# A two-layer hybrid block: the written order counts transfers on the load queue, large loads come in pieces, and the first transfers go through one queue

## The chip, the cores and the metric

The kernel runs on one core of a Trainium2 chip. A core has a matrix engine (TensorE, here PE, with its weight loads shown apart as PEld), a vector engine (VectorE, DVE), an activation engine (ScalarE, ACT), GpSimd (POOL) and SyncE (SP), which in this kernel issues nearly all transfers. Each engine runs its own instructions in the order in which the program wrote them and waits on semaphores for the others. Transfers run on 16 DMA engines. The metric is the device time of one execution in microseconds (us); lower is better. "Granted clock" is the share of its full clock that PE was given.

## The reference: what is computed

Two layers are applied to a sequence of 256 rows of width 1024, then a final RMS norm. A layer normalises its input, projects it with one wide matrix, and runs three branches on the parts:

```
h = rms_norm(x); proj = h @ w_in           # 1024 x 14352
y_a = differential attention: 8 heads, RoPE, causal softmax, a = p0 - lam * p1, norm, * silu(z), @ w_o
y_c = u = a * sigmoid(g); depthwise causal convolution of 31 taps; layer_norm; silu * silu(z); @ w_o
y_d = short convolution of 4 taps, silu, l2 norm; gated delta rule, 8 heads of 128;
      norm, * silu(z), @ w_o
x = x + (g_a * y_a + g_c * y_c + g_d * y_d) @ w_out     # gates: sigmoid of three parts of proj
```

All of it is float32. The gated delta rule solves a unit lower triangular system for each chunk of the sequence and head; the kernel inverts its 16x16 diagonal blocks first and goes on from there with matrix products.

## The kernel before

**Dense products.** All large weights are cut into groups of 512 columns, and each group into four chunks of 512 KB (`w_raw`, 128 partitions x 1024). SP loads a chunk (`load`, L423), ACT rounds it to `w_hi` (`prepare`, L430), DVE takes the rest as `w_lo` (`lows`, L442), and PE multiplies three times: high by high, high by low, low by high. There are three buffers of each of the three tiles. A chunk's load is issued when `w_lo` of the chunk three before it has been taken, since only then is its raw buffer free. `dense` (L477) runs one group: four chunks, and between their matmuls it calls `pump` (L365).

**How the order of the work is set.** The program writes all instructions of a layer in one pass, and a small planner chooses their order. A clock `clk[0]` counts the time of PE's matmuls by fixed costs; `busy` has the time up to which DVE, ACT and GpSimd are filled. Side work is a set of generators, each a `Stream` (L284) with a priority. A stream's `yield` closes a run of steps. `serve` (L301) writes the stream's next step when its inputs should be there by the planner's clock. For a transfer, `dma` (L356) takes a number, the time after which the planner believes that the data has landed, and a plain `yield 8.0` sets the start of the run of steps that it closes 8 us later. For weights, `load` notes `clk[0] + 4.5` as the landing. No two transfers know of each other in this account. Once written, the order is fixed: if a transfer lands later than the planner thought, the engine that needs it stands, and all that is written behind it on that engine stands too.

**The order of groups.** `SEQ` (L60) lists the steps of the projection phase: `v` the attention values, `k` the delta-rule keys, `q` its queries, `w` its values, `x` the start of its solve, `c` the two convolution groups, `d` a block of the long convolution, `a` attention queries and keys, `z` a gate, `t` the RoPE tables. The digit is the half (or the block for `d`). Behind them come, for the delta branch, the attention and the convolution in turn, gate groups (`g`) and output products (`y`) as `PHASE` lists them: for the delta branch g0, g1, y0, y1. The four convolution blocks are 256 channels each: block 0 runs on DVE as scaled adds over time (`conv_steps`, L1132), blocks 1 to 3 on PE (`conv_group`, L1163).

**Block copies.** `dn_keys` (L878) makes the 16x16 diagonal blocks of one half of the heads (`vc`), stores them to DRAM (`v_keep`, 64 KB) and reads them back so that each partition holds all 16 rows of its block: `nrep`, two copies of 512 KB, on a tile named `y_hi` in the first half of the heads and `t8` (shown as `t`) in the second. Then DVE runs the inverse: 15 steps, of which step i reads the rows 0 to i of `nrep`, into `dn_z`, with `dn_t` as room. GpSimd spreads `dn_z` (POOL, `t<-dn_z`), PE transposes it, and the solve goes on. The SP engine waits for the store to land before the copies, as they read what it wrote.

**Convolution loads.** `evac_u` (L1113) makes 512 of the convolution's input channels, stores them to DRAM (`u_keep`, 512 KB) and, for the first half, starts `conv_load(1)` (L1147): the taps as a block of matrices (`wd`, 1 MB), then `u4` (shown as `u`), the input four times, shifted by 0 to 3 steps, 256 KB each, read from `u_keep`. `conv_group(n)` starts `conv_load(n + 1)` when its matmuls have been written.

**The start.** x comes transposed (`xt`, four transfers of 256 KB): three on ACT's queue and one on SP's; the weights come on SP's. ACT issues the transfers of four constants before its first activation. `first_part` (L610) scales two slices of x, `prepare(2)` takes the first chunk in two halves, and then the dense work of the first group begins.

## Time and profile before

| | us |
|---|---|
| median of 3 runs | 1114.2 (1113.66 to 1120.59) |
| profiled execution, its own time | 1114.95 |
| its span, first to last instruction | 1113.2 |
| PE busy | 1044.5 |
| DVE busy | 866.7 |
| ACT busy | 548.3 |
| mean granted clock | 0.971 |

The profile is of one execution. Times in it count from its first instruction. A row of a timeline gives start, length, engine, line, operation and operands; in square brackets stands the idle time of the engine before it and what ended it. "SPq" and "ACTq" are transfers issued by these engines, and their length is that of the issue, not of the transfer. "DMA y_hi<-v_keep" as the end of a wait is the landing of that transfer. A row of the view by stretch gives the stretch, its length, the busy time of PE, PEld, DVE, ACT and POOL (with the number of instructions), the granted clock, the DMA engines' busy share and GB/s. Almost all vector and activation work bears line 130, that of a helper, so the tile names tell it apart.

### The profile page before, as it was taken

Reading aid. Unit: us, or ns where it says so; the run is one execution under the profiler, and the core shown is the slowest. Engines: PE = TensorE matmul, PEld = TensorE weight load, DVE = VectorE, ACT = ScalarE, POOL = GpSimd, SP = SyncE. Lnnn points to the kernel's source line nnn. Section 1 sums busy time; section 2 is a strip of 40 time slices with the busy share of each in tenths; the row PEclk is TensorE's granted clock in tenths of the full one; section 3 lists DMA queues with packets and bytes.
Section 4 is the critical chain, followed back from the end, with each engine's and each line's share of the span. In section 5 each row is a group of like instructions: output and inputs, shape, how many; then the busy total and the mean of one; then the engine's idle time right before and its main releaser. Section 6 shows DMA issues by size and latency. Waiting matters only on the chain.

```text
span 1113.2 us, 18028 instructions
## 1 busy us (share of the span) xinstructions
PE 1044.5 (94%) x6892; PEld 905.1 (81%) x6892; DVE 866.7 (78%) x1729; ACT 548.3 (49%) x977; POOL 102.3 (9%) x73
## 2 busy tenths in 40 slices
PE   6999759989999999999999998998989999999996
PEld 5899747889877888897889998788978777879885
DVE  4799657769766899996578979876877579989855
ACT  4564325334544556554456553534354355665543
POOL 0001001300010000121100200030000000002220
PEclk8999878989999999999999998999989999999998
DMA  6555573244535456556665566634443535645662
GB/s 215 160 163 165 177 191 114 97 135 133 159 111 148 133 172 206 169 187 193 185 206 168 153 197 213 179 114 133 135 134 110 137 117 168 212 150 174 198 207 82
DMA packets 57894, 178.07 MB, mean 160 GB/s; under 512 B 6480, under 2 KB 16336, under 8 KB 57040
## 3 DMA queue, kind: packets, MB, share of 16 engines
q1 hardware_dynamic: 56240, 175.17, 52.0%
q10 hardware_dynamic: 1568, 1.75, 0.5%
q8 instruction: 54, 0.88, 0.3%
q14 instruction: 32, 0.26, 0.1%
HBM read 172.44 MB, written 4.46 MB: 159 GB/s over the span
## 4 chain that ended last, share of the span: by engine, by line
PE 69%; DVE 17%; DMA 8%; issue 3%; ACT 2%; SPq 0%; ACTq 0%; DVEq 0%
PE acc L349 55%; PE s L347 11%; DVE w_lo L130 6%; DMA w_raw<-in_wts 4%; PE s L354 3%; DVE big L130 2%; DMA y_hi<-v_keep 1%; DMA t<-v_keep 1%; ACT w_hi L130 1%; DVE c_acc L130 1%; DVE vv L130 1%; DVE gx L130 1%; DMA big<-in_x_t 1%; DVE dn_t L130 1%; DMA u_keep<-c_u 0%
## 5 line engine op out<-in xcount | busy, mean ns | idle before, releaser
L130 ACT CAST w_hi<-w_raw 128x1024 fp32r<-128x1024 f32 (+1 forms) x289 | 302.3, 1046 | 354.7 <-PE acc L349 235.7
L130 DVE TENSOR_TENSOR w_lo<-w_raw,w_hi 128x1024 fp32r<-128x1024 f32 (+1 forms) x289 | 365.5, 1266 | 77.7 <-ACT w_hi L130 76.8
L349 PE MATMUL acc<-h_hi,w_lo 128*128 128x256 f32 x768 | 220.5, 287 | 14.3 <-DVE w_lo L130 14.1
L349 PE MATMUL acc<-h_hi,w_hi 128*128 128x256 f32 x768 | 224.5, 292 | 0.0
L349 PE MATMUL acc<-w_hi,h_hi 128*128 128x512 f32 x512 | 216.0, 422 | 6.6 <-ACT w_hi L130 6.6
L349 PE MATMUL acc<-h_lo,w_hi 128*128 128x256 f32 x768 | 219.3, 286 | 0.0
L349 PE MATMUL acc<-w_lo,h_hi 128*128 128x512 f32 x512 | 202.0, 395 | 0.6 <-DVE w_lo L130 0.6
L349 PE MATMUL acc<-w_hi,h_lo 128*128 128x512 f32 x512 | 202.2, 395 | 0.0
L349 PEld LDWEIGHTS acc<-h_hi,w_lo 128*128 128x128 f32 x768 | 149.4, 195 | 16.1 <-DVE w_lo L130 15.9
L349 PEld LDWEIGHTS acc<-h_hi,w_hi 128*128 128x128 f32 x768 | 149.7, 195 | 1.4 <-issue 1.0
L349 PEld LDWEIGHTS acc<-h_lo,w_hi 128*128 128x128 f32 x768 | 149.6, 195 | 0.3
L349 PEld LDWEIGHTS acc<-w_hi,h_hi 128*128 128x128 f32 x512 | 97.7, 191 | 26.0 <-ACT w_hi L130 6.8
L349 PEld LDWEIGHTS acc<-w_hi,h_lo 128*128 128x128 f32 x512 | 97.1, 190 | 21.7 <-DVE h_lo L130 0.2
L349 PEld LDWEIGHTS acc<-w_lo,h_hi 128*128 128x128 f32 x512 | 98.0, 191 | 17.0 <-DVE w_lo L130 1.9
L130 DVE SCALAR_TENSOR_TENSOR c_acc<-c_u,pc,c_acc 128x255 f32<-128x255 f32 (+29 forms) x120 | 51.3, 470 | 2.3 <-ACT c_acc L130 2.3
L349 PE MATMUL acc<-w_hi,y_lo 128*128 128x512 f32 x128 | 50.1, 391 | 2.0 <-DVE y_lo L130 2.0
L349 PE MATMUL acc<-w_hi,y_hi 128*128 128x512 f32 x128 | 51.5, 402 | 0.3 <-ACT y_hi L130 0.3
L349 PE MATMUL acc<-w_lo,y_hi 128*128 128x512 f32 x128 | 49.9, 390 | 0.0
L130 DVE SCALAR_TENSOR_TENSOR big<-wc,pc,big 128x255 f32<-128x255 f32 (+2 forms) x96 | 47.6, 543 | 0.5 <-ACT big L130 0.5
L349 PE MATMUL acc<-u,wd 128*32 128x256 f32 (+7 forms) x768 | 41.7, 369 | 1.8 <-ACT c_acc L130 1.8
L349 PE MATMUL acc<-w_hi,t 128*128 128x512 f32 x128 | 40.0, 389 | 0.0
L349 PEld LDWEIGHTS acc<-u,wd 128*32 128x32 f32 x768 | 23.7, 110 | 18.3 <-ACT c_acc L130 3.5
(276 smaller groups left out, 1521.1 us busy)
## 6 DMA issues: line engine op xcount, KB each, us to landing
w_raw<-in_wts SPq DMA_DIRECT2D x287, 512.0 KB, 3.8
wd<-in_cwd SPq DMA_DIRECT2D x6, 1024.0 KB
y_hi<-v_keep SPq DMA_DIRECT2D x4, 512.0 KB
u_keep<-c_u SPq DMA_DIRECT2D x4, 512.0 KB, 5.3
t<-v_keep SPq DMA_DIRECT2D x4, 512.0 KB
u<-u_keep SPq DMA_DIRECT2D x6, 256.0 KB, 6.4
u<-u_keep SPq DMA_DIRECT2D x6, 255.0 KB, 7.3
u<-u_keep SPq DMA_DIRECT2D x6, 254.0 KB, 7.2
```

What stands on the lines that cost most here:

```text
L130: step = (self.key, lambda: getattr(self.eng, op)(*args, **kw), cost)
L347: live[0].steps.append(("PE", lambda: TE.matmul(**kw), cost))
L349: TE.matmul(**kw)
L354: ("PE", lambda: TE.transpose(out=out, in_=in_, identity=ident[0:n, 0:n]), 0.11))
```

## The change

**Account of the queue.** `dma` takes a size and a rate in place of a landing time. `transfer` keeps two times: `lane[0]`, when SP is free to issue (0.45 us an issue), and `lane[1]`, when the queue has moved all that was asked (1.2 us from issue at the earliest, then size by rate, 280 GB/s if nothing else is said); landing is 0.6 us later. Weight loads go through the same account. A stream whose last step is a transfer is done at its landing, so `until` on it waits for that.

**Block copies.** Four copies of 256 KB in place of two of 512 KB, each a stream of its own, written some 1.8 us apart from right behind the store on; the inverse waits for the landing of each quarter before step 4, 8 and 12 (and before its first step for the first). Their rate in the account is 130 GB/s.

**Convolution loads.** `conv_load` is now started behind the second convolution group, at a high priority. The taps come in four transfers of 256 KB, 1.5 us apart; the four shifted inputs are 2 us apart, and begin at the landing of the stored half.

**Order of groups.** `d1`, block 1 of the convolution, stands behind `w1` and `x1`. Block 3 (`last_conv`, L1483) stands behind the delta branch's first product (`y`) instead of its first gate group.

**First transfers.** x and the first chunks go through SP's queue in the order x 0-1, weights 0a, x 2-3, weights 0b, weights 1, x 4-7, weights 2. The four constants are issued by ACT behind its work on the first two chunks.

```
@@ -57,7 +57,7 @@
     PHASE[k] = (("g", 0), ("g", 1), ("y", 0), ("y", 1))
-SEQ = "v0 k0 t0 z0 k1 v1 q0 w0 c0 x0 q1 a0 d1 w1 x1 c1 z1 a1 d2".split()
+SEQ = "v0 k0 t0 z0 k1 v1 q0 w0 c0 x0 q1 a0 w1 x1 d1 c1 z1 a1 d2".split()
 TAPQ = 8
@@ -225,8 +225,6 @@
     xt = act.tile([P, KT, T], F32, name="big", bufs=3)
-    for k in (0, 2):
-        nc.scalar.dma_start(out=xt[:, k:k + 2], in_=x_t[:, k:k + 2])
     S.activation(out=one, in_=ones[:, 0:1], func=AF.Square)
@@ -284,7 +282,7 @@
             self.gen, self.prio, self.steps, self.held, self.marks = gen, prio, [], [], False
-            self.t, self.on, self.over, self.done, self.read = clk[0], "", False, False, None
+            self.t, self.on, self.over, self.done, self.read, self.land = clk[0], "", False, False, None, 0.0
@@ -310,6 +308,7 @@
                         self.done = True
+                        self.t = max(self.t, self.land)
                         streams.remove(self)
@@ -330,7 +329,8 @@
                     else:
-                        self.t = clk[0] + cost
+                        self.land = max(self.land, transfer(due, *cost))
+                        self.t = lane[0]
                     self.on = key
@@ -353,8 +353,16 @@
-    def dma(landing, **kw):
-        live[0].steps.append(("SP", lambda: nc.sync.dma_start(**kw), landing))
+    def dma(kb, rate=280.0, **kw):
+        live[0].steps.append(("SP", lambda: nc.sync.dma_start(**kw), (kb, rate)))
+    def transfer(due, kb, rate=280.0):
+        lane[0] = max(lane[0], due, clk[0]) + 0.45
+        lane[1] = max(lane[1], lane[0] + 1.2) + kb * 1.024 / rate
+        return lane[1] + 0.6
+    lane = [0.0, 0.0]
@@ -420,12 +428,14 @@
-    def load():
+    def load(freed=0.0):
         if len(raws) < len(queue):
...
                 nc.sync.dma_start(out=raw[:, kk], in_=wts[queue[len(raws)]][:, kk])
-            raws.append((raw, clk[0] + 4.5))
+                if not raws and not kk:
+                    nc.sync.dma_start(out=xt[:, 2:4], in_=x_t[:, 2:4])
+            raws.append((raw, transfer(freed, 512)))
@@ -447,7 +457,7 @@
             if kk.stop == KC:
-                load()
+                load(ready[n][2])
@@ -644,15 +654,12 @@
+    nc.sync.dma_start(out=xt[:, 0:2], in_=x_t[:, 0:2])
     load()
-    nc.scalar.dma_start(out=xt[:, 4:6], in_=x_t[:, 4:6])
     load()
-    nc.sync.dma_start(out=xt[:, 6:8], in_=x_t[:, 6:8])
+    nc.sync.dma_start(out=xt[:, 4:8], in_=x_t[:, 4:8])
     load()
-    nc.scalar.dma_start(out=cst[:, 0:CO_NW], in_=consts[:, 0:CO_NW])
-    nc.scalar.dma_start(out=cst[:, CO_TRI:CO_N], in_=consts[:, CO_TRI:CO_N])
-    nc.scalar.dma_start(out=pat, in_=patt)
-    nc.scalar.dma_start(out=pos_i, in_=positions.rearrange("b (c p) -> p (b c)", p=P))
+    lane[0] = lane[1] = 9.5
     idle = side[0][0]
@@ -665,9 +672,13 @@
     prepare()
-    clk[0] = 6.5
+    clk[0] = 6.0
     s_f = add(first_half())
     s_r = [(1, s_f)]
+    nc.scalar.dma_start(out=cst[:, 0:CO_NW], in_=consts[:, 0:CO_NW])
+    nc.scalar.dma_start(out=cst[:, CO_TRI:CO_N], in_=consts[:, CO_TRI:CO_N])
+    nc.scalar.dma_start(out=pat, in_=patt)
+    nc.scalar.dma_start(out=pos_i, in_=positions.rearrange("b (c p) -> p (b c)", p=P))
     s_q = add(first_squares(), 0.1)
@@ -924,22 +935,39 @@
             st["gam"], st["ngam"], st["nk"] = gam, ngam, nk
-            dma(3.5, out=v_keep[hs], in_=vc.rearrange("p c h i -> p (c h i)"))
-            yield 3.5
-            for half in range(2):
-                dma(0.1 if half else 7.0, out=nrep[:, 8 * half:8 * half + 8].rearrange("p j c i -> p (j c i)"),
-                    in_=v_keep[hs].rearrange("(b h j) n -> h b (j n)", b=8, h=2)[half].unsqueeze(1).to_broadcast(
-                        [8, 16, 8 * P]))
-            yield 8.0
+            dma(64, out=v_keep[hs], in_=vc.rearrange("p c h i -> p (c h i)"))
+            yield 0.1
+            def blocks(n):
+                dma(256, 130.0, out=nrep[:, 4 * n:4 * n + 4].rearrange("p j c i -> p (j c i)"),
+                    in_=v_keep[hs].rearrange("(b h j) n -> h b (j n)", b=8, h=4)[n].unsqueeze(1).to_broadcast(
+                        [8, 16, 4 * P]))
+                yield
+            def copies():
+                for n in range(4):
+                    s_b.append(add(blocks(n), 0.05))
+                    yield 1.8
+            s_b = []
+            add(copies(), 0.05)
+            while not s_b:
+                yield
+            yield from until(s_b[0])
             z = sm.tile([P, 8, 16], F32, name="dn_z", bufs=1)
...
             for i in range(1, 16):
+                if i % 4 == 0:
+                    yield
+                    while len(s_b) <= i // 4:
+                        yield
+                    yield from until(s_b[i // 4])
                 t1 = sm.tile([P, 8, 16], F32, name="dn_t1", bufs=1)
...
                 V.tensor_reduce(out=z[:, :, i:i + 1], in_=t1[:, :, 0:i + 1], axis=AX.X, op=ALU.add)
-                if i % 3 == 0 or i == 7:
-                    yield 6.0 if i == 7 else None
+                if i % 4 == 1:
+                    yield
             if hs == 0:
@@ -1117,15 +1145,15 @@
                 yield
-                dma(3.0, out=u_keep[s * GW:(s + 1) * GW].rearrange("(a p) t -> p a t", p=P), in_=us[s])
-                stored.append(s)
+                yield from ()
+                dma(512, out=u_keep[s * GW:(s + 1) * GW].rearrange("(a p) t -> p a t", p=P), in_=us[s])
                 if s == 0 and NV:
                     taps_left[0] = conv_steps()
-                if s == 0 and NV < 2:
-                    s_cv[NV] = add(conv_load(NV))
             s_g = group_a(l, ("in", CG + s * GW), H, evac_g)
-            group_a(l, ("in", CA + s * GW), H, evac_u)
+            stored.append(group_a(l, ("in", CA + s * GW), H, evac_u))
+            if s == 0 and NV < 2:
+                s_cv[NV] = add(conv_load(NV), 0.05)
@@ -1145,13 +1173,19 @@
         def conv_load(n):
-            dma(0.1, out=wd.rearrange("p f q j c -> p (f q j c)"), in_=cwd[l, n - NV])
+            for f in range(2):
+                for q in range(2):
+                    qs = slice(4 * q, 4 * q + 4)
+                    dma(256, out=wd[:, f, qs].rearrange("p q j c -> p (q j c)"),
+                        in_=cwd[l, n - NV].rearrange("p (f q x) -> p f q x", f=2, q=2)[:, f, q])
+                    yield 1.5
             while len(stored) <= n // 2:
                 yield
-            yield 3.0
+            yield from until(stored[n // 2])
             for i in range(4):
-                dma(0.1 if i < 3 else 6.0, out=u4[32 * i:32 * i + 32, :, i:T],
+                dma(256, 150.0, out=u4[32 * i:32 * i + 32, :, i:T],
                     in_=u_keep[n * 2 * P:(n + 1) * 2 * P, 0:T - i].rearrange("(g c) t -> c g t", c=32))
+                yield 2.0
@@ -1176,7 +1210,7 @@
             if n < 3:
-                s_cv[n + 1] = add(conv_load(n + 1))
+                s_cv[n + 1] = add(conv_load(n + 1), 0.05)
@@ -1481,7 +1515,7 @@
         def last_conv(kind, i):
-            if kind == "g" and not i:
+            if kind == "y" and not i:
                 conv_group(3)
```

## The prediction

> **What bounds the kernel now.** I read the totals of the page first, then the stretches in which TensorE (PE) stands still, then who it waits for, then the load queue. The totals:
>
> ```profile
> PE 1044.5 (94%) x6892; PEld 905.1 (81%) x6892; DVE 866.7 (78%) x1729; ACT 548.3 (49%) x977; POOL 102.3 (9%) x73
> ```
>
> PE is the bound over most of the span, so only what PE loses can be won. The view of busy time by stretch shows where it loses it (stretch, its length, then PE busy first; granted clock, DMA share and GB/s last). These seven stretches hold the larger gaps behind the start:
>
> ```profile
> 124.00:132.00 8.00, 1.31 (x9) 1.10 (x8) 3.17 (x9) 1.04 (x1) 0.00 (x0) 0.71 0.33 109
> 150.00:170.00 20.00, 5.58 (x19) 3.94 (x18) 8.65 (x16) 5.33 (x9) 2.41 (x2) 0.62 0.45 123
> 240.00:246.00 6.00, 1.97 (x14) 1.77 (x13) 1.73 (x8) 3.36 (x14) 0.00 (x0) 0.78 0.53 144
> 665.00:673.00 8.00, 1.48 (x10) 1.28 (x9) 4.05 (x13) 1.32 (x2) 0.00 (x0) 0.81 0.30 102
> 702.00:706.00 4.00, 2.11 (x12) 1.54 (x11) 1.64 (x3) 2.72 (x4) 0.00 (x0) 1.00 0.51 204
> 773.00:780.00 7.00, 2.69 (x22) 2.48 (x20) 2.06 (x9) 1.04 (x1) 0.00 (x0) 0.95 0.49 151
> 814.00:819.00 5.00, 1.45 (x10) 1.24 (x9) 4.59 (x16) 2.62 (x5) 0.00 (x0) 0.78 0.73 268
> ```
>
> Length less PE busy gives the idle time: 6.69, 14.42, 4.03, 6.52, 1.89, 4.31 and 3.55 us. A gap is dearer than its length, since the granted clock falls to half behind most of them. The same view over the half-clock stretches (the first belongs to the start):
>
> ```profile
> 7.83:14.66 6.83, 3.37 (x7) 2.44 (x8) 4.10 (x7) 4.84 (x10) 0.00 (x0) 0.50 0.69 238
> 127.30:134.13 6.83, 2.96 (x14) 2.96 (x15) 5.23 (x14) 0.00 (x0) 0.00 (x0) 0.50 0.39 133
> 154.61:175.09 20.48, 9.50 (x30) 7.61 (x31) 13.28 (x24) 7.89 (x14) 2.41 (x2) 0.50 0.28 93
> 243.35:250.18 6.83, 5.00 (x23) 5.01 (x24) 4.20 (x11) 0.10 (x1) 0.00 (x0) 0.50 0.45 139
> 670.02:676.85 6.83, 4.71 (x22) 4.71 (x23) 6.69 (x14) 1.23 (x2) 0.00 (x0) 0.50 0.45 146
> 779.25:782.66 3.41, 3.41 (x18) 3.41 (x17) 3.31 (x10) 0.00 (x0) 0.00 (x0) 0.50 0.06 22
> 816.79:823.62 6.83, 5.42 (x25) 4.72 (x25) 4.17 (x10) 4.03 (x8) 0.00 (x0) 0.50 0.40 140
> ```
>
> Work done at half clock would have taken half the time, so each row loses half of its PE busy time. Now who is waited for (waits of PE):
>
> ```profile
> PE acc L349 <- DVE w_lo L130: 14.7, 6, 6.7
> ```
>
> The engine named is only the last link. VectorE (DVE) works in written order, and its timeline shows what holds it:
>
> ```profile
> 128.66 0.19 DVE L130 TENSOR_TENSOR dn_t<-dn_z,y_hi 128x16 f32<-128x16 f32 x1 [8.75 <-DMA y_hi<-v_keep]
> ```
>
> The inverse of the 16x16 blocks was written before its block copies had landed; `w_lo`, which PE needs, stands behind it. Asked for the scratch tensor `v_keep`, the trace gives all four such waits, two a layer:
>
> ```profile
>   DVE dn_t L130: 28.7, 4
> ```
>
> 28.7 us of DVE waits became 6.69 + 4.03 + 6.52 + 4.31 = 21.55 us of PE gaps: a wait is absorbed for (28.7 - 21.55) / 4 = 1.8 us, and the rest shows. The other large gap (150 to 170) comes from the load queue; SyncE's (SP) timeline:
>
> ```profile
> 109.12 0.42 SPq L357 DMA_DIRECT2D v_keep<-dn_vc  x1
> 112.24 7.50 SPq L427 DMA_DIRECT2D w_raw<-in_wts  x4
> 119.79 1.35 SPq L357 DMA_DIRECT2D y_hi<-v_keep  x2
> 131.15 8.04 SPq L427 DMA_DIRECT2D w_raw<-in_wts  x4
> 139.23 0.43 SPq L357 DMA_DIRECT2D u_keep<-c_u  x1
> 139.71 0.51 SPq L357 DMA_DIRECT2D wd<-in_cwd  x1
> 144.53 2.16 SPq L357 DMA_DIRECT2D u<-u_keep  x4
> 146.79 1.53 SPq L427 DMA_DIRECT2D w_raw<-in_wts  x3
> ```
>
> At 139.71 SP puts the whole 1 MB of taps on the queue, then waits at the `u` loads until 144.53, when the `u_keep` store has landed (5.3 us after its issue at 139.23). No weight is asked for until 146.79, and those three weight loads are queued behind 2 MB. ScalarE (ACT) then waits up to 12 us for a weight:
>
> ```profile
> ACT w_hi L130 <- DMA w_raw<-in_wts: 51.3, 24, 12.0
> ```
>
> **Block copies, in four pieces and counted.** Gone: 21.55 us of PE gaps and half of 2.96 + 5.00 + 4.71 + 3.41 us of half-clock work, 8.0 us; together 29.6 us. The old order issues the copies 10.7 us after the store (109.12 to 119.79) and starts the inverse at once; the new one issues the first copy right behind the store and starts the inverse at the modelled landing of its quarter. The added wait is SP's: it stands at the first copy until the store of 64 KB has landed. That landing is not in the trace; the nearest rows are the 512 KB store above, 5.3 us, and the weight load:
>
> ```profile
> w_raw<-in_wts SPq DMA_DIRECT2D x287, 512.0 KB, 3.8
> ```
>
> I take 3.8, as the store is small, so SP stands for about 3 us (2 to 5), and the weight loads behind it, one each 2.5 us by the SP rows (7.50 us for x4, three intervals), come that much late. Of this 1.8 us is absorbed. That leaves 0 to 3 us at each of four places; I take 1.1, in all 4.4. What is late next is seen in busy time by stretch again, where five rows serve this part and those below:
>
> ```profile
> 60.00:260.00 200.00, 173.96 (x1327) 159.92 (x1326) 155.99 (x321) 84.87 (x145) 19.20 (x14) 0.91 0.50 148
> 600.00:820.00 220.00, 203.73 (x1553) 187.42 (x1552) 183.35 (x377) 102.18 (x178) 23.59 (x16) 0.97 0.55 164
> 640.00:660.00 20.00, 20.00 (x167) 19.82 (x166) 19.79 (x38) 12.64 (x19) 0.00 (x0) 1.00 0.67 192
> 141.00:146.00 5.00, 5.00 (x44) 5.00 (x43) 4.72 (x14) 2.10 (x2) 0.00 (x0) 1.00 0.99 376
> 122.00:130.00 8.00, 2.48 (x21) 2.27 (x19) 1.17 (x7) 1.68 (x2) 0.00 (x0) 0.83 0.45 150
> ```
>
> The copies move slowly (150 GB/s at 122 to 130 with DMA share 0.45, against 376 with 0.99 at 141 to 146), so the last quarter is late next; but the inverse reads quarter after quarter.
>
> **Convolution loads in pieces.** Gone: the gaps of 14.42 and 1.89 us and half of 9.50, 4.7 us; together 21.1 us. The `u` loads now wait for the modelled landing of the store, 0.45 + 1.2 + 1.87 + 0.6 = 4.1 us by the diff's constants for 512 KB, so SP still stands 5.3 - 4.1 = 1.2 us, under the 1.8 that is absorbed. The queue has room: its share is 0.50 and 0.55 in the two long stretches. Residue over six such loads: 0 to 2 us each, of which I take 0.7, in all 4. The pieces add 18 tap loads and 8 copies; at 0.51 us and 1.35 / 2 us of issue these are 15 us of SP, spread over ten places and hidden while SP is ahead of PE.
>
> **First transfers.** PE's first dense matmul and what ACT did before it:
>
> ```profile
> 11.29 0.80 PE L349 MATMUL acc<-w_hi,h_hi 128*128 128x512 f32 x1 [6.59 <-ACT w_hi L130]
> ```
> ```profile
> 9.38 0.39 ACTq L655 DMA_DIRECT2D pos_i<-in_positions  x1
> 9.82 0.91 ACT L130 ACTIVATE h_hi<-big,cst 128x256 fp32r<-128x256 f32 x2 [6.17 <-DMA big<-in_x_t]
> ```
>
> ACT reaches its first activation only behind the last constant's issue. With the constants behind the first weights, and 256 KB of x and 256 KB of weights, together the size of one weight load, first in one queue, the first operands are there at about 5.0 us: 3.8 behind two issues of 0.42 and some 0.4 before the first, an estimate. From ACT's first activation to PE's first matmul it took 11.29 - 9.82 = 1.5, so PE starts at about 6.5, and up to 4.8 us and the 3.37 / 2 = 1.7 us of half clock could go. But the next chunks still have to come through the queue, so I take 3 (0 to 6). The four constant issues, 0.39 us each by the row above, now stand between ACT's weight copies, covered by the chunks ready by then; uncovered they cost 1.6 us.
>
> **Convolution blocks 1 and 3 later.** Block 1 goes behind w1 and x1, block 3 from behind the first gate of the delta branch to behind the branch's first product; with block 1 the loads of block 2 move on SP's queue. The matmuls are moved, not removed. Here the stretch of block 1's old place, that block's matmuls alone:
>
> ```profile
> 198.00:207.00 9.00, 6.95 (x128) 3.96 (x128) 1.00 0.35 102
> ```
>
> None of the seven gaps lies there and the queue is at 0.35, so block 1 covers nothing and its move costs nothing. Block 3 is another matter: it gives 6.95 us in which the branch's output gets ready, and that ends only just in time (VectorE's row, then PE's first use):
>
> ```profile
> 371.94 0.75 DVE L130 SCALAR_TENSOR_TENSOR y_lo<-s,nwc,y_hi 128x512 fp32r<-128x512 f32 x1
> ```
> ```profile
> 372.72 0.39 PE L349 MATMUL acc<-w_hi,y_hi 128*128 128x512 f32 x1
> ```
>
> 371.94 + 0.75 is 372.69. With block 3 gone from ahead of it, PE is there up to 6.95 us sooner. For a smaller price: the inverse, the solve's first part, starts some 10 us earlier against the store. So 0 to 6.95 us in each layer; I take 1.5, in all 3.
>
> The gap of 3.55 us at 814 has DVE at 4.59 of 5.00 us: DVE is the bound there, no transfer, and I leave it standing. An order written anew will put some operations too early elsewhere: 3 us (-6 to 8).
>
> **Sum.** 1114.95 (profiled execution; its span is 1113.2, and 1.75 lies around it) - 29.6 - 21.1 - 3 + 4.4 + 4 + 3 (block 3) + 3 (new order) = 1075.65. The median of the runs is 0.75 below the profiled one: 1075.
>
> A residue also matters to the clock. PE's row behind the gap of 3.55 us:
>
> ```profile
> 818.20 1.20 PE L347 MATMUL s<-dn_vo,gf 128*128 128x128 f32 x4 [3.55 <-DVE gf L130]
> ```
>
> PE fell idle at 818.20 - 3.55 = 814.65, and the last half-clock row has the clock down from 816.79, 2.1 us later. So residues above some 2 us would cost half of up to 6.83 us more. The Trainium skill ("TensorE: Matmul & The Clock Gate", Part 1: The HAM clock gate) lets the clock fall after an idle window of about 3.4 us. By that rule residues of 2 to 3.4 us are free of it and the sum is unchanged; by the row each costs up to 3.4 us more, which is within the range. The trace does not agree with the rule's full idle window.
>
> **The rivals.** A: DVE takes over as the bound. In 60 to 260 PE loses 25.14 us idle and 8.73 by clock; without them the stretch is 166.1 us and DVE's 155.99 are 94% of it. In 600 to 820, 12.72 and 4.06 go, leaving 203.2, and DVE's 183.35 are 90%. Against: at 640 to 660 DVE is at 19.79 of 20.00 and PE still at 20.00. For: long stretches show 78% and 83% now. Half-way, at 86%, the stretches take 181.4 and 213.2 us, so 25.4 go, with the start 28.4: 1086. Chance 0.22.
>
> B: the order still doesn't keep clear of the transfers (its constants are a model, and SP's wait for the store isn't in it): the copies' 29.6 us stay, half of the 21.1 goes: 1114.95 - 10.5 - 3 + 3 - 0.75 = 1104. For it: copies at 150 GB/s, below the model's 280 for all else. Against: the inverse is now held for each quarter. Chance 0.10.
>
> C, slower: the 26 added transfers each pay their fixed part on the queue, and the weights behind them are late. 3.8 us for 512 KB, of which 1.4 at 376 GB/s, leaves 2.4 us; 26 x 2.4 = 62 us, and 1075 + 62 = 1137. It decides when pieces follow one another without overlap. Against it: 376 GB/s at share 0.99 with several transfers in flight. Chance 0.06. The Trainium skill speaks for it ("DMA: Bandwidth & Descriptors", Bandwidth): batch transfers to 1 MiB or more; with the fixed 2.0 us a transfer that its section "Anatomy of one DMA" gives for the gpsimd path, these 26 would make 52 us, an estimate. The row of 141 to 146 does not bear it out for overlapping transfers.
>
> **How the numbers follow.** The forecast case, most of both groups gone, has 0.62. It reaches from 1054 (no residue, and the 3.55 us gap and its half clock gone too: 1114.95 - 53.7 - 6.3 - 0.75) to about 1090, with the bounds of block 3 and the new order; A fills 1080 to 1100. With B and C left out, and the edges cut a little, the range is 1055 to 1098. A measurement of this kernel tells about 1% from no change, 1103 to 1125. Faster: forecast and nearly all of A, 0.83. Same: B and the rest of A, 0.11. Slower: C, 0.06.
>
> **What would show it.** Copies: the waits on `v_keep` fall from 28.7 us to under 8, PE gaps at those four places under 2 us, no half clock there. Convolution: ACT's waits for `w_raw` fall from 51.3 to under 30, no weight pause on SP near the first `u` loads. Start: first dense matmul before 8.5 us. A would show as DVE at 95% or more with PE gaps behind DVE work, B as `v_keep` waits above 15 us, C as `w_raw` landing medians well above 3.8 us with ACT waiting on them. The prediction falls if the gaps go and others of the same size come at places where nothing stood.

## The result and the profile after

The kernel after takes 1084.41 us (median of 4 runs, 1082.1 to 1086.07), against 1113.93 for the kernel before: a ratio of 0.9726 (95% interval 0.9676 to 0.9775), 2.7% faster. The prediction was 1075 (1055 to 1098). The profiled execution took 1082.91, its span is 1081.1 and its mean granted clock 0.985; 32.1 us of span are gone. One of the four executions of the kernel with block 3 back, below, took 1302.31 us at a granted clock of 0.746 (the other three 0.974 to 0.977), so its time and its profile are left out (an expectation below that speaks of 15 us for block 3 still counts it). The totals on the page of after:

```profile
PE 1038.0 (96%) x6892; PEld 899.1 (83%) x6892; DVE 876.4 (81%) x1729; ACT 547.6 (51%) x977; POOL 103.9 (10%) x73
```

Busy time by stretch (columns as before). The first row is the first copies and inverse of layer 0, the second its convolution loads, the third the copies of its second half; the fourth and fifth the copies of layer 1, and the last two the long stretches that rival A was worked out from:

```profile
108.00:126.00 18.00, 13.12 (x88) 12.42 (x87) 13.58 (x38) 5.03 (x6) 0.00 (x0) 0.81 0.67 202
135.00:160.00 25.00, 24.36 (x173) 22.13 (x172) 21.70 (x35) 16.07 (x28) 2.84 (x2) 1.00 0.61 181
195.00:245.00 50.00, 50.00 (x476) 45.90 (x465) 43.70 (x104) 23.87 (x51) 2.99 (x2) 1.00 0.53 158
636.00:652.00 16.00, 9.59 (x57) 9.10 (x56) 13.82 (x38) 5.22 (x6) 0.00 (x0) 0.68 0.73 208
725.00:790.00 65.00, 65.00 (x581) 58.50 (x580) 51.91 (x124) 32.86 (x77) 3.06 (x2) 1.00 0.48 142
60.00:260.00 200.00, 193.65 (x1508) 178.53 (x1507) 177.58 (x354) 98.19 (x165) 25.30 (x16) 0.98 0.57 171
600.00:820.00 220.00, 212.34 (x1612) 193.96 (x1611) 190.02 (x389) 103.56 (x193) 21.76 (x16) 0.98 0.57 161
```

Five of the seven old gaps are gone (the fifth row also holds the place of the gap that stood at 814, which the prediction had left standing; from 652 to 725 us, with the convolution loads of layer 1, PE is idle for 1.26 us in all). The two at the copies of the first half of the heads are not: 4.88 and 6.41 us idle. Half-clock stretches between start and end:

```profile
117.78:124.61 6.83, 4.85 (x21) 4.56 (x22) 5.54 (x14) 4.07 (x5) 0.00 (x0) 0.50 0.51 156
271.38:274.79 3.41, 3.41 (x12) 2.83 (x11) 2.02 (x3) 0.27 (x1) 0.00 (x0) 0.50 0.05 12
640.02:650.26 10.24, 6.02 (x26) 5.73 (x27) 9.11 (x22) 3.48 (x4) 0.00 (x0) 0.50 0.70 206
872.13:875.54 3.41, 3.41 (x14) 2.82 (x12) 2.81 (x10) 1.84 (x5) 0.00 (x0) 0.50 0.24 95
```

DVE waits less for the copies (first line: us, times, from the view of the scratch tensor), yet ACT waits longer for weights (second line: us, times, the longest):

```profile
  DVE dn_t L130: 11.1, 7
```
```profile
ACT w_hi L130 <- DMA w_raw<-in_wts: 61.4, 34, 9.8
```

What is left shows at the first copies. SP's timeline, then ACT's, then PE's:

```profile
99.35 3.32 SPq L435 DMA_DIRECT2D w_raw<-in_wts  x2
102.73 0.42 SPq L357 DMA_DIRECT2D v_keep<-dn_vc  x1
106.36 1.97 SPq L357 DMA_DIRECT2D y_hi<-v_keep  x3
108.85 0.34 SPq L435 DMA_DIRECT2D w_raw<-in_wts  x1
109.24 1.29 SPq L357 DMA_DIRECT2D y_hi<-v_keep  x1
110.64 12.30 SPq L435 DMA_DIRECT2D w_raw<-in_wts  x4
```
```profile
117.66 1.04 ACT L130 CAST w_hi<-w_raw 128x1024 fp32r<-128x1024 f32 x1 [9.84 <-DMA w_raw<-in_wts]
```
```profile
118.76 0.58 PE L349 MATMUL acc<-h_hi,w_hi 128*128 128x256 f32 x1 [3.65 <-ACT w_hi L130]
120.56 0.58 PE L349 MATMUL acc<-h_hi,w_lo 128*128 128x256 f32 x1 [1.00 <-DVE w_lo L130]
```

From the issue of the store to the first copy 3.6 us pass (102.73 to 106.36), 3.2 of them SP's wait for the store to land; then SP issues three copies at once. The pause of 1.8 us that was to keep them apart has no effect: it closes a run without steps, and the copies leave SP 0.6 to 1.5 us apart. No weight is asked for between 102.67 (99.35 + 3.32) and 108.85, and the one asked for then is there only at 117.66, 8.8 us later, where the median is 3.7: three copies are ahead of it and one right behind, 1 MB in all. So ACT waits 9.84 us for a weight, and PE behind it. In layer 1 the first copy goes out 5.0 us behind the store, 4.5 of them SP's wait, and PE's gaps are 4.88 and 1.53.

**The balance.** With idle time and half of the half-clock work counted as loss, the first-half copies cost 3.65 + 1.00 + 4.85 / 2 = 7.1 and 4.88 + 1.53 + 6.02 / 2 = 9.4, together 16.5 us. Two losses stand where nothing stood: 1.23 + 2.38 + 3.41 / 2 = 5.3 us in the solve (the 1.23 at 260.61), and 0.93 + 1.51 + 3.41 / 2 = 4.1 where block 3 had been:

```profile
270.36 1.13 PE L347 MATMUL s<-dn_r,t 128*128 128x128 f32 x8 [2.38 <-DVE dn_r L130]
869.29 0.50 PE L349 MATMUL acc<-w_hi,y_hi 128*128 128x512 f32 x1 [0.93 <-ACT y_hi L130]
871.53 0.50 PE L349 MATMUL acc<-w_hi,y_lo 128*128 128x512 f32 x1 [1.51 <-DVE y_lo L130]
```

Gone are 29.6 at the copies, 21.1 at the convolution loads, 6.3 at 814 (3.55 + 5.42 / 2) and 3.8 at the start (below). 60.8 gone less 25.9 new is 34.9, against 32.1 of span. Of the missing 2.8 us, 1.9 is work: PE busy less half of its half-clock work is 1027.3 us before and 1029.2 after. The rest lies in smaller gaps.

### The profile page after: what moved, and what is told of

Its sections match the earlier page's. It is cut to its first block, busy times and chain, and to the rows that moved or that the text cites. A ratio compares the mean times of both kernels' runs of the same rounds, so it can differ in the third digit from the quotient of the medians.

```text
span 1081.1 us, 18074 instructions
## 1 busy us (share of the span) xinstructions
PE 1038.0 (96%) x6892; PEld 899.1 (83%) x6892; DVE 876.4 (81%) x1729; ACT 547.6 (51%) x977; POOL 103.9 (10%) x73
## 4 chain that ended last, share of the span: by engine, by line
PE 73%; DVE 16%; DMA 5%; issue 3%; ACT 2%; SPq 0%; DVEq 0%; ACTq 0%
PE acc L349 59%; PE s L347 11%; DVE w_lo L130 6%; PE s L354 3%; DMA w_raw<-in_wts 2%; DVE big L130 2%; DMA y_hi<-v_keep 2%; DVE c_acc L130 2%; ACT w_hi L130 1%; DVE gx L130 1%; DVE wa L130 1%; DVE dn_vc L130 1%; DVE tz L130 0%; DMA cst<-in_consts 0%; DMA v_keep<-dn_vc 0%
## 5 line engine op out<-in xcount | busy, mean ns | idle before, releaser
L349 PE MATMUL acc<-w_hi,h_hi 128*128 128x512 f32 x512 | 212.4, 415 | 3.5 <-ACT h_hi L130 2.0
L130 DVE SCALAR_TENSOR_TENSOR big<-wc,pc,big 128x255 f32<-128x255 f32 (+2 forms) x96 | 51.3, 577 | 0.0
L130 POOL TENSOR_TENSOR wa<-wa 128x512 f32<-128x512 f32 x16 | 23.3, 1456 | 207.4 <-DVE wa L130 181.4
```

Of the source, the lines that this page charges most:

```text
L130: step = (self.key, lambda: getattr(self.eng, op)(*args, **kw), cost)
L349: TE.matmul(**kw)
```

## The experiments

Each edit is against the kernel after, "-" what stands there, "+" what the experiment has. Each kernel computes the whole reference. Ratios are to the kernel before, with 95% intervals; kernels whose intervals overlap are not told apart by time alone. Differences in us are between medians. The kernel before, run again beside each group of experiments, had medians from 1113.93 to 1118.11 us, so where it matters the difference by ratios (times 1113.93) stands beside.

### One part taken back at a time

**Block copies as before.**

```
-            dma(64, out=v_keep[hs], ...); yield 0.1     # four copies of 256 KB, inverse waits for each quarter
+            dma(64, out=v_keep[hs], ...); yield 3.5
+            for half in range(2):
+                dma(512, 130.0, out=nrep[:, 8 * half:8 * half + 8]..., in_=v_keep[hs]...)
+            yield 8.0                                   # inverse yields at i % 3 as before
```

> The changed kernel with the block copies alone as they were: two of 512 KB, the inverse started with their issue, the old pauses. Theory (each removed stall has its own price, and the copies brought a net 13 us: 29.6 us of old loss less 16.5 us of new loss at the two places in the first half of the heads): about 1097 us, DVE waits on v_keep back at 25 us or more. Rival (the new account of the queue alone keeps the order clear of the transfers, and the pieces only move the stall from DVE to the weight loads): 1081 to 1088 us.

1086.78 us, 0.9759 (0.9705 to 0.9813): 2.4 us above the change as a whole (intervals overlap), not the 29.6 less 16.5 that the stalls would make it. Waits of DVE on the copies:

```profile
  DVE dn_t L130: 15.6, 3
```

The rest of the change takes the wait at the old copies from 28.7 to 15.6 us (the account alone, below, to 20.7); the new copies bring it to 11.1 but stand in the way of weights. PE has a gap of 4.87 us at 231.05 (for `dn_r`) that the change doesn't have.

**Convolution loads as before.**

```
-            for f in range(2):                          # taps in four pieces, 1.5 us apart
-                for q in range(2): ... dma(256, ...); yield 1.5
-            yield from until(stored[n // 2])
+            dma(1024, out=wd..., in_=cwd[l, n - NV])
+            yield 3.0
                 dma(256, 150.0, out=u4[...], ...)
-                yield 2.0
                                                         # conv_load started in evac_u again, old priority
```

> The changed kernel with the convolution loads alone as they were: 1 MB of taps at once, the four shifted inputs in a row and 3 us behind the store, started where they were. Theory (the pieces are worth the 21.1 us of old gaps behind them, and nothing of that was given back): about 1105 us, with ACT waits of 8 us or more for w_raw behind the first such load and a PE gap there. Rival (the account of the queue is enough to place work around one large burst): 1084 to 1091 us.

1086.14 us, 0.9749 (0.9706 to 0.9792): 1.7 us more (intervals overlap), where 21 had been expected. SP, then ACT at the same place:

```profile
139.13 0.45 SPq L357 DMA_DIRECT2D wd<-in_cwd  x1
141.93 1.81 SPq L357 DMA_DIRECT2D u<-u_keep  x4
143.85 21.16 SPq L435 DMA_DIRECT2D w_raw<-in_wts  x6
```
```profile
148.56 1.05 ACT L130 CAST w_hi<-w_raw 128x1024 fp32r<-128x1024 f32 x1
154.75 1.05 ACT L130 CAST w_hi<-w_raw 128x1024 fp32r<-128x1024 f32 x1 [1.49 <-DMA w_raw<-in_wts]
```

The 2 MB go out in one burst as before, but ACT has chunks in hand when it starts: from 139.31 up to 148.56 it takes three chunks without waiting for a transfer. The first wait is 1.49 us and the largest gap of PE there 2.67.

**The start as before.** x on two queues, the constants ahead of ACT's first activation.

```
+    for k in (0, 2): nc.scalar.dma_start(out=xt[:, k:k + 2], ...)
-    nc.sync.dma_start(out=xt[:, 0:2], ...); load(); load()
-    nc.sync.dma_start(out=xt[:, 4:8], ...); load()      # constants behind prepare() of two chunks
+    load(); nc.scalar.dma_start(out=xt[:, 4:6], ...); load()
+    nc.sync.dma_start(out=xt[:, 6:8], ...); load()      # the four constants right here
```

> The changed kernel with the first transfers alone as they were: x on ACT's queue in three transfers, constants ahead of ACT's first activation. Theory: PE's first dense matmul at 11.3 us instead of 6.4, but 2 us of that is lost again by PE waiting for the next chunks, so the whole costs 3 us: about 1087 us. Rival 1: all of the 4.9 us and the half clock behind it stay, 1091 us. Rival 2: the gap at 24 us, before the first norm, takes it all up, 1084 us.

1089.70 us, 0.9782 (0.9739 to 0.9825), 5.3 more (intervals overlap); the first dense matmul is back at 11.19.

**Block 3 and block 1 at their old places.**

```
-            if kind == "y" and not i:
+            if kind == "g" and not i:
                 conv_group(3)
```

> The changed kernel with convolution block 3 back behind the delta branch's first gate group. Theory: its 6.95 us gave the branch's output time to get ready; the gaps of 0.93 and 1.51 us and the half clock behind them at the branch's first product in layer 1 go, about 4 us: 1080 us. Rival: the block's place is of no account, since what covers one wait uncovers another: 1083 to 1088 us.

1097.86 us (three executions), 0.9864 (0.9811 to 0.9918): 13.5 more, though a gain of 4 had been expected. Without a profile the place of the loss isn't known here; the run of the old place with the old loads, below, says more.

```
-SEQ = "... q1 a0 w1 x1 d1 c1 z1 a1 d2".split()
+SEQ = "... q1 a0 d1 w1 x1 c1 z1 a1 d2".split()
```

> The changed kernel with convolution block 1 back in front of w1. Theory of the prediction (the place covers nothing): 1082 to 1087 us. Rival (as with block 3, the loads in paced pieces, 14 us of planned time behind the stored half, are not there at the old place, and PE waits for them as written): 1090 to 1100 us, with a gap or a stretch of half clock at the block in layer 0 or 1.

1080.43 us, 0.9652 (0.9602 to 0.9702): 4 us less (8 by ratios), within what the intervals leave open. The profiled spans are equal, 1080.8 and 1081.1 us, and PE has next to no idle time around block 1 at either place (170 to 215 us: 0.23 us in this kernel, 0.43 after the change; 710 to 750 us: 0.59 and 0.06). So the profiles show no worth of the new place; the times leave open that the old one is a little better.

### Two parts together

**The account of the queue alone**, all else as in the kernel before (sizes and rates in `dma`, `transfer`, `load`).

```
-                        self.t = clk[0] + cost          # before; the account, as in the change:
+                        self.land = max(self.land, transfer(due, *cost)); self.t = lane[0]
```

> The kernel before with the account of the queue alone: transfers known by size and rate, weights in the same account, and every transfer issued in the old pieces, from the old queues and places. Theory now (taking the pieces away one kind at a time cost 2 us each, so the written order that knows of landings carries most of the gain): 1090 to 1100 us, waits on v_keep about 15 us as without the new copies, and no gap above 5 us behind the convolution's burst. Rival (pieces and account do the same work twice, and one without the other is worth little: either alone holds off the stalls only together with the new places): above 1105 us.

1114.89 us, 0.999 (0.9961 to 1.0019): no gain, where 14 to 24 had been expected. Waits on the copies, and the stretch in which the convolution loads hold up the weights:

```profile
  DVE dn_t L130: 20.7, 4
```
```profile
148.00:158.00 10.00, 5.42 (x18) 3.81 (x17) 8.79 (x15) 4.75 (x7) 2.63 (x2) 0.69 0.42 140
```

The wait on the copies is shorter, but 4.58 us are still idle in this stretch alone, at a clock of 0.69. Over the span PE's idle time up to its last matmul falls from 58.3 to 49.6 us (all its gaps added) while its half-clock work rises from 34.4 to 46.8 (all such rows but the last), which takes half of 12.4 us back. That large loads are known to the order doesn't help here, where they still go out whole. But the count of the copies' landing isn't used here either: the inverse is written as soon as the copies are issued, as before, and DVE stands for them:

```profile
129.75 0.19 DVE L130 TENSOR_TENSOR dn_t<-dn_z,y_hi 128x16 f32<-128x16 f32 x1 [5.25 <-DMA y_hi<-v_keep]
```

That the inverse waits for the counted landing came with the pieces. Whole copies with such a wait were not tried, so this run doesn't tell what the account is worth with it.

**Old copies and old convolution loads**, both edits above.

> The changed kernel with both the block copies and the convolution loads as they were; account, start and places new. Theory 1 (each of the two is worth its own 2 to 4 us): 1088 to 1091 us. Theory 2 (they stand in for each other: a stall at the copies empties the reserve of weights, and the burst of convolution loads 15 us later is only dear where the reserve is empty, so one of the two is enough): 1095 to 1105 us, with a gap above 5 us between 130 and 165 us.

1104.22 us, 0.9858 (0.9799 to 0.9917): 19.8 more than the change (14.7 by ratios), where the parts alone make 2.4 and 1.7 (3.7 and 2.6). The profiled spans agree: 23.7 us more, against 3.6 and 4.1. PE's gaps are 3.26 us from 127.28 on, behind the copies, then 1.68 from 138.91, 2.48 from 149.11 and 2.38 from 152.10: the one gap over 5 us that had been expected didn't come in one piece. SP and ACT:

```profile
134.44 0.50 SPq L357 DMA_DIRECT2D wd<-in_cwd  x1
138.51 1.81 SPq L357 DMA_DIRECT2D u<-u_keep  x4
140.59 18.24 SPq L435 DMA_DIRECT2D w_raw<-in_wts  x6
```
```profile
134.26 1.05 ACT L130 CAST w_hi<-w_raw 128x1024 fp32r<-128x1024 f32 x1 [8.86 <-DMA w_raw<-in_wts]
...
150.50 1.04 ACT L130 CAST w_hi<-w_raw 128x1024 fp32r<-128x1024 f32 x1 [10.73 <-DMA w_raw<-in_wts]
```

The same burst of taps and inputs, but it starts when ACT has just waited 8.86 us for a weight behind the old copies: little is in hand, and two chunks later a weight makes it wait 10.73. With the old loads and the new copies the copies' stall stands too (a gap of 4.38 us up to 119.77), but 19 us ahead of the burst, and ACT has chunks in hand again; with the old copies and the new loads no burst follows. That the parts stand in for each other is shown by the times and spans; that the reserve of weights is how, is read from these rows, for layer 0.

**Old convolution loads, block 3 at its old place.** Both edits above.

> The changed kernel with the convolution loads as they were and block 3 back at its old place. Theory: block 3 back alone cost 15 us because its loads in paced pieces take 4 x 1.5 + 4 x 2.0 = 14 us of planned time and a gate group gives 11; with the loads at once they fit, so 1083 to 1090 us. Rival: the place itself costs 15 us, by the order that follows from it: about 1100 us.

1094.36 us, 0.9801 (0.9768 to 0.9835): 8.2 above the old loads at the new place (intervals overlap), against 13.5 with the paced loads. By the medians the old place costs more when the loads are paced, so the pieces are likely part of why block 3 had to move, but not all of it. The trace shows what else the old place costs: the gaps in front of the delta branch's first product are gone, as had been expected, but in the attention of layer 1 PE has gaps of 2.54 and 4.88 us (up to 966.23 and 972.26), the second for DVE (`big`), which is busy for 11.06 of the 12.00 us from 962 to 974.

**The account without its queue, old copies.** Each transfer counted by itself:

```
-        lane[0] = max(lane[0], due, clk[0]) + 0.45
-        lane[1] = max(lane[1], lane[0] + 1.2) + kb * 1.024 / rate
-        return lane[1] + 0.6
+        lane[0] = max(due, clk[0]) + 0.45
+        return lane[0] + 1.2 + kb * 1.024 / rate + 0.6
```

> The changed kernel with the old block copies, and with an account in which transfers don't queue: each has its own 0.45 + 1.2 us, its size by its rate, and 0.6 us, whatever else is on the queue. To be held against the kernel with the old copies alone, 1086.8 us. Theory (given the pieces and places, the queue in the account still decides where weights are thought late): 1093 us or more. Rival (the account's queue is of no account, as it was without the pieces, where it brought 0 us): 1083 to 1090 us.

1099.03 us, 0.982 (0.9771 to 0.9869), against 1086.78 for the old copies with the queue: 12 us by the medians, 7 by ratios, with overlapping intervals. What the queue in the account is worth given the pieces is likely above the nothing that the account is worth alone, but not shown. It wasn't tried with the new copies, nor with weights alone left out of the account.

### What is left at the first copies

Three edits of one line: the `yield` that closes a copy's run, and so sets the pause in front of the copy. Each kernel has one of the "+" lines:

```
             def blocks(n):
                 dma(256, 130.0, out=nrep[:, 4 * n:4 * n + 4]...
-                yield
+                yield 4.0                               # late
+                yield 2.7 * n if n and not hs else None # paced0
+                yield None if hs else 4.0 + 1.2 * n     # late0_spaced
```

**All copies 4 us later than the store** (weights can be asked for while the store lands).

> The changed kernel with the four block copies 4 us later behind the store, all four alike. Theory (SP stands at the first copy until the store has landed, 3.6 us and 5.0 us at the two places that still stall, and the weight loads behind it come late): with one or two weight loads written ahead of the copies, the gaps of 3.65 + 1.00 and 4.88 + 1.53 us and the half clock behind them, 16 us in all, fall to less than half: about 1075 us. Rival (what delays the weights is 1 MB of copies ahead of them on the DMA engines, whenever it is issued): 1082 to 1087 us, with the same gaps.

1079.48 us, 0.9684 (0.9657 to 0.9711), 4.9 less (intervals overlap). PE's gaps at the first halves are 0.42, 0.76, 0.56 and 2.61, then 1.60 and 0.78 us; a new one of 4.04 stands in layer 1's solve from 783.51 on. SP waits for the store for only 1.3 and 1.1 us, but the copies still come two at a time in layer 0 and four at a time in layer 1. With the half clock behind 2.61 and 1.60 us (3.41 us of work each), 4.34 + 2.39 + 3.41 = 10.1 us are left at the two places of what is, counted in the same way, 4.88 + 6.41 + 5.4 = 16.7 in the change: not less than half, as had been expected.

**The first half's copies 2.7 us apart by the planner's clock, the first at once** (the weight loads come between).

> The changed kernel with the copies of the first half of the heads 2.7 us apart (as written, the pause of 1.8 us between them has no effect on their issue: they leave SP 0.7 to 1.5 us apart), the first one at once. Theory of the queue (the copies ahead of the weights are the delay): a weight load goes between any two copies, and the gaps at the two places fall to less than half: about 1076 us. Theory of SP's stand: the stand is still there, so the gaps stay: 1082 to 1087 us.

1077.62 us, 0.9659 (0.9636 to 0.9682). DVE's waits on the copies rise to 15.1 us in 6, as quarters come later, but no gap at the first copies is over 2 us, and no half clock is there. 5.03 + 4.15 = 9.2 us are left of the 16.7, though SP still waits for the store, 2.9 and 3.1 us (3.2 and 4.5 in the change). So the stand is not the whole of it: weight loads between the copies help with the stand in place.

**Both, in the first half alone.**

> The changed kernel with the copies of the first half of the heads begun 4 us behind the store and 1.2 us apart by the planner's clock, so that a weight load stands ahead of the first and between the first three; the second half's copies are left alone. If SP's stand behind the store and the copies ahead of the weights are two parts of the same 16 us: 1071 to 1077 us, the gaps at the two places together under 4 us and no half clock there. If either was all of it, nothing is gained over the two kernels that took one away: 1076 to 1080 us.

1072.90 us, 0.959 (0.9541 to 0.9638): faster than the change (0.9726, 0.9676 to 0.9775) and than the kernel before. SP at the first copies, and PE in the two stretches:

```profile
104.74 0.42 SPq L357 DMA_DIRECT2D v_keep<-dn_vc  x1
106.70 0.33 SPq L435 DMA_DIRECT2D w_raw<-in_wts  x1
108.28 0.73 SPq L357 DMA_DIRECT2D y_hi<-v_keep  x1
110.20 0.34 SPq L435 DMA_DIRECT2D w_raw<-in_wts  x1
110.59 0.61 SPq L357 DMA_DIRECT2D y_hi<-v_keep  x1
111.98 1.31 SPq L435 DMA_DIRECT2D w_raw<-in_wts  x1
113.33 1.32 SPq L357 DMA_DIRECT2D y_hi<-v_keep  x2
```
```profile
108.00:130.00 22.00, 19.06 (x154) 18.45 (x154) 18.89 (x44) 9.91 (x12) 0.00 (x0) 1.00 0.71 192
640.00:655.00 15.00, 12.14 (x99) 11.74 (x99) 14.21 (x36) 6.73 (x9) 0.00 (x0) 1.00 0.68 201
```

A weight load goes out while the store lands, and one behind each of the first two copies. DVE waits 2.9 us for the copies, in 3. PE's idle time at the two places falls from 4.88 + 6.41 to 2.94 + 2.86 us (under 4 in all had been expected), and the clock stays at 1.00. That makes 5.5 us of gaps and, by the two half-clock rows of after, 5.4 of clock: 10.9 in all. The span fell by 10.1, with 5.1 lost by the clock at the start (last section); the remainder, some 4 us gained, lies elsewhere. One edit leaves 10.1 us at these places, the other 9.2, both together 5.8. So SP's stand and the copies ahead of the weights were behind some two thirds of the 16.7 us that the change had left there.

## Why the prediction was right

It was right in sign and range, and 9 us below the median. None of the rivals came, but of its likeliest case, both groups of stalls mostly gone, only the half on the convolution: at the copies 29.6 us went and 16.5 came back. That the median lies no further off is in part luck: 6.3 us went at a place that was to be left standing, without which it would be some 1091.

- **Block copies: right that they go, the residue mis-sized.** The waits on `v_keep` fell to 11.1 us, not under 8; the gaps were under 2 us, without half clock, at two of the four places only. "SP stands for about 3 us (2 to 5)" held, at 3.2 and 4.5 in the first halves. The step that failed is the next one, "Of this 1.8 us is absorbed. That leaves 0 to 3 us at each of four places": it counted the stand alone. Three copies stand ahead of the next weight load on SP, and that load took 8.8 us beside them, 8.0 in layer 1. The term was 4.4 and measured 16.5, all of it in the first halves, 5.4 of it half clock, which the term left out. The prediction had the row for the copies' slow 150 GB/s, but used it for the last quarter and not for the weight behind the copies. The second halves, with four copies in a row behind the store, lost nothing: the weights asked for around them (191.01 to 199.75, and 729.01 to 735.81) are taken by ACT only 14 to 16 us later, when PE has freed a buffer, so a late landing doesn't show there.
- **Convolution loads: right.** 21.1 us gone and the 4 of residue didn't come: 0.64 us idle in the row of 135.00 to 160.00. SP's pauses near the `u` loads (150 to 170 us) all wait for `w_lo` to free a buffer, none for the store. But that this is the price of the part was wrong: taken back alone it costs 1.7 us. The sum of stalls was better as a total than as a list of prices: taken back together with the copies it costs 19.8.
- **The start: right.** The first dense matmul, and the first 30 us before and after:

```profile
6.37 0.49 PE L349 MATMUL acc<-w_hi,h_hi 128*128 128x512 f32 x1 [1.53 <-ACT w_hi L130]
```
```profile
4.80:30.00 25.20, 15.89 (x69) 12.46 (x69) 14.79 (x33) 12.72 (x22) 0.00 (x0) 0.86 0.65 216
4.80:30.00 25.20, 17.99 (x94) 14.25 (x94) 17.62 (x43) 14.08 (x23) 0.00 (x0) 1.00 0.73 238
```

6.5 had been predicted. After has 17.99 us of PE work at clock 1.00, against 15.89 of which 3.37 at half clock: 17.99 - 15.89 + 3.37 / 2 = 3.8 us gained by 30 us, where 3 was taken (5.3 by the experiment, whose interval overlaps). Of the 4.9 us by which PE starts sooner and the 1.7 of half clock, 2.8 go again, in new waits, the largest 0.76 us for `w_lo` (up to 11.10) and 2.01 us for `h_hi` (up to 20.00).

- **Block 3 and block 1.** 4.1 us of loss where the prediction put 3 for block 3, for the cause it gave: PE is early for the delta branch's output (rows of 869.29 and 871.53), in layer 1 alone. What it didn't see is what the move buys: at the old place the whole takes 13.5 us more. That block 1's move costs nothing fits the profiles; the times leave some us open.
- **New order and the gap at 814.** 5.3 us of loss at the place shown, where 3 was taken, and the 6.3 at 814 went, which were left standing because "DVE is the bound there". In the order written anew PE never waits for `gf`, DVE's output there; the choice to leave the gap was wrong by 6.3 us.
- **ACT's waits for weights** were to fall from 51.3 to under 30 and rose to 61.4. They are 34 in place of 24, the longest 9.8 us in place of 12.0. The new copies seem to be what adds to them: with the old copies alone they are 43.1 us, with the old convolution loads alone 65.2. But 43.1 goes with 1086.78 us, 43.6 with the fastest kernel, and 68.3 with 1077.62 (copies 2.7 us apart), so their sum was the wrong thing to watch.
- **The rivals.** A: DVE is at 177.58 of 193.65 us of PE's busy time in the first long stretch (92%) and at 190.02 of 212.34 in the second (89%); PE's two largest gaps there, 3.65 and 4.88 us, end with ACT, and the later runs went below A's 1086, to 1072.9. It came near in places: from 148 to 172 us DVE is busy for all of the 24.00 us, and PE still for 23.15. B: `v_keep` waits 11.1, under its 15. C: the landing of a weight didn't rise with 26 more transfers:

```profile
w_raw<-in_wts SPq DMA_DIRECT2D x287, 512.0 KB, 3.7
```

The rule of the Trainium skill to batch transfers to 1 MiB or more ("DMA: Bandwidth & Descriptors", Bandwidth) doesn't show as a cost here: the weights' median is 3.7 us as against 3.8, and the kernel with taps of 1 MB is not faster (1086.14). A quarter of the taps itself, 256 KB, lands in 4.8 us at the median.

In total the losses that came back were 14.4 in the sum and 25.9 on the chip; the gap at 814 and the start made up 7.1 of it. The 4.4 left over and the 2.8 of the balance are the 7.2 us by which the span lies above the sum's 1075.65 - 1.75 = 1073.9. The prediction was to fall if gaps of the same size came where nothing had stood; the two that came, 5.3 and 4.1 us in all, are well below those that went.

## What to carry to other kernels

On a queue of just-in-time weights, a group of transfers that reads back a store cost twice here, once while the queue stood and once while the weight behind the group was late: put weight loads into the time of the landing, and between the pieces. Stalls that feed on one reserve have no prices that add up: either part of the change alone seemed worth 2 us when taken back, both 15 to 20, so undo parts in pairs before calling one useless. The account of the queue earned nothing by itself; whether it needs small pieces, or readers that wait for the counted landing, is left open by these runs.

## What had not been expected of the hardware

**The clock goes by fixed windows.** Changes of the granted clock come at multiples of 3.41 us from one another, and a gap costs the clock only where enough of it lies in one window. The same matmuls on `wc` wait 2.67 us in the kernel after and in the one with the account alone, whose half-clock row stands third:

```profile
26.79 0.61 PE L347 MATMUL s<-ones,wc 128*128 128x1 f32 x4 [2.67 <-DVE wc L130]
```
```profile
29.61 0.80 PE L349 MATMUL s<-ones,wc 128*128 128x1 f32 x3 [2.67 <-DVE wc L130]
```
```profile
28.86:35.69 6.83, 6.08 (x28) 6.08 (x29) 5.44 (x19) 1.04 (x1) 0.00 (x0) 0.50 0.48 157
```

In after the border of 25.62 (117.78 - 27 x 3.4133) splits the gap into 1.50 and 1.17 us, and the clock stays. In the other 1.92 us of the gap lie ahead of the border of 28.86, and two windows at half clock follow. In before and after together every window at full clock with 2.09 us idle or more was followed by half clock, and none with 1.50 or less was (each worked out from PE's gaps and the changes of the clock). In the experiments some falls came behind windows with as little as 1.0 us, so the bound isn't sharp, or the modelled ends of matmuls blur it. The Trainium skill ("TensorE: Matmul & The Clock Gate", Part 1: The HAM clock gate) has a free-running window of this length, which the trace bears out, and names an idle window for the fall, where some 2.1 us of it are enough here.

**The same start has its clock by chance.** In after no half clock shows between 5 and 30 us; in the fastest kernel, with the same code there, three windows do:

```profile
7.81:11.22 3.41, 3.41 (x10) 2.65 (x9) 2.36 (x5) 2.01 (x4) 0.00 (x0) 0.50 1.02 374
21.46:24.87 3.41, 3.41 (x15) 3.12 (x14) 3.31 (x11) 2.46 (x6) 0.00 (x0) 0.50 0.35 131
28.29:31.70 3.41, 3.41 (x18) 3.41 (x17) 3.03 (x15) 1.05 (x1) 0.00 (x0) 0.50 0.64 184
```

That is 3 x 3.41 / 2 = 5.1 us between two executions, more than the 3.8 us that the new start gains by the profile, so one profile can't price it. The borders of the windows lie elsewhere against the first instruction (7.81 as against 8.55), and the windows ahead of the three have 1.82, 2.33 and 1.41 us idle, where after has 1.50 at the most.
